# Key pages from GpSimd's DMA queue with the keys dealt eight ways, value pages from the sync engine's

## The chip, the core and the metric

The kernel runs on one core of a Trainium2 chip. A core has a matrix engine (TensorE, PE in the profile, with its weight loads as PEld), a vector engine (VectorE, DVE), an activation engine (ScalarE, ACT), a general engine (GpSimd, POOL), and a sync engine (SP), which here only issues DMAs. DMAs issued from SP, ACT and POOL run on the core's 16 DMA engines and move data between HBM and the on-chip memory of 128 partitions (SBUF). The metric is the device time of one execution in microseconds; lower is better.

## What is computed

One step of a two-layer decoder trunk: layer 0 has stick-breaking attention, layer 1 a diagonal state-space layer; each is followed by a gated MLP with a short convolution. The same weights serve a prompt of 512 tokens and 8 sample sequences of 8 new tokens. The change is in the attention of the samples, whose past of 2048 tokens lies in pages of 128 keys and values:

```python
def stick_breaking_block(q, k, v, bias, q_start):
    z = einsum("bqhd,bkhd->bhqk", q, k) * HEAD_DIM ** -0.5 + bias
    causal = k_pos[None, :] < q_pos[:, None]
    log_keep = where(causal, log_sigmoid(-z), 0.0)
    between = cumsum(log_keep, axis=3, reverse=True) - log_keep
    weights = where(causal, exp(log_sigmoid(z) + between), 0.0)
    return einsum("bhqk,bkhd->bqhd", weights, v)
...
past_kv = [(cache_k[j][page_table].reshape(db, n_pages * PAGE_SIZE, N_HEADS, HEAD_DIM),
            cache_v[j][page_table].reshape(db, n_pages * PAGE_SIZE, N_HEADS, HEAD_DIM))
           for j in range(N_ATTN)]
```

8 sequences, 16 pages each, 128 keys a page, 16 heads of 64: each page is 512 KB of keys and 512 KB of values in fp32, so 67 MB of keys and 67 MB of values are read.

## The kernel before

The sequences are taken in pairs. `sample_cache` (L395) is a generator that walks over 64 steps: 4 pairs, and in each the 16 pages from the last to the first. A step takes one page of both sequences. Its parts are these.

- `load_k` (L406) loads the keys of a step into a tile `kp` of 128 partitions x 4 x 512 floats, two of them (`KBUF`). For each sequence s it reads the page number into a register (`page_id`, L390) and issues two DMAs, one for each half j of the heads, from the sync engine. Each writes 32 partitions, starting at 32 * (2 * j + s): partition kk of the group takes the four keys 4 * kk to 4 * kk + 3. The source's dimensions are 32 x 4 x 512.
- `load_v` (L417) loads the values of a step into a tile `vp` of 128 partitions (one key each) x 2 x 1024 floats, two of them (`VBUF`), with two DMAs from GpSimd. A `vp` buffer comes free when the matmul `po` (L483) of two steps before has read it.
- `turn` (L424) transposes `kp` on VectorE in blocks of 32 x 32 (L427), in two calls a step; after the second, the buffer is free and the keys of two steps on are issued.
- z (L448): 32 matmuls a step with the queries as weights. The output is written so that z's columns are in the order of the keys: out of a column (b, k) to column 4 * k + b.
- ScalarE takes two sigmoids of z, VectorE a reversed running product over the keys and a multiply (`sg`, L464), PE transposes the weights (L473), and `po` (L483) accumulates the weighted values over the 16 pages.

This stream of steps is woven into the prompt's work: `accompany(stream, WEAVE)` lets it take one of its four parts a step after every 2400 columns of the prompt's matmuls. It begins in the first projections (L768), runs beside the prompt's attention (8 pairs of heads, `project_pair`, `norm_pair`, `prompt_pair`) and is finished in the output projection and the first MLP.

The sync engine also issues all weight loads (`load_unit`, L151, its DMA on L168) into three buffers `raw`; ScalarE and VectorE split each into a high and a low part, the first few on GpSimd (`GUNITS`, L140). It issues the prompt's stores as well. An engine issues its DMAs in the order of its program, and one that waits for a buffer holds up those behind it. A scheduler puts each engine's program in order at build time; `tc.issue_after(x)` adds that what is issued in its block on x's engine comes after x. With `raws["last"]` such an order is kept among the weight loads: after the first key loads it is set to the last of their DMAs (L771, `RL` is 2), so that the head pairs' weights come after them on the sync engine.

Of the kernel before, what the change touches and what calls it, by code (L numbers as in the profile page):

```python
# [17 lines left out]
P = 128  # L18
# [35 lines left out]
SB = {"gemm": 3, "tr": 2, "vy": 3}  # L54
SHARE = {"up": "vy"}
EARLY = 2
RL = 2
XA, XB = 0, 2
RAWU = 3, 4
QGROUPS = [[0, 1], [2, 3]]  # L60
# [31 lines left out]
def hybrid_kernel(  # L92
# [9 lines left out]
    V, S, G, T, SP = nc.vector, nc.scalar, nc.gpsimd, nc.tensor, nc.sync  # L102
# [46 lines left out]
    raws = {"pool": glob, "bufs": NRAW, "n": -1, "last": None, "chain": True, "views": {}}  # L149
# [50 lines left out]
    def norm_rows(xs, rows, gain, room=rows_tile, inplace=False):  # L200

        hs = [room()] * len(xs) if inplace else [room() for x in xs]
        ss = const.tile([P, len(xs)], F32, name="ss", tag="ss", bufs=3)
        for i, x in enumerate(xs):
            S.activation(hs[i][:rows], x, AF.Square, accum_out=ss[:rows, i:i + 1])
        r = rsqrt(const, ss, len(xs), rows, 1.0 / D, "nr", 3)
        if inplace:
            hs = xs
        for i, x in enumerate(xs):
            V.scalar_tensor_tensor(hs[i][:rows], x, r[:rows, i:i + 1], gain[:rows], ALU.mult, ALU.mult)  # L210
        return hs
# [86 lines left out]
    def attention_layer(sp, sps):  # L298
# [54 lines left out]
        Qall = sp.tile([P, DB // 2, 16, 32], F32, name="Qall", bufs=1)  # L353
# [34 lines left out]
        last_dma = {}  # L388

        def page_id(eng, idx):  # L390

            with tc.issue_after(last_dma[eng].ins) if eng in last_dma else nullcontext():
                return eng.value_load(idx, min_val=0, max_val=cache_k.shape[1] - 1)

        def sample_cache():  # L395

            steps = [(b, m) for b in range(DB // 2) for m in range(NPG - 1, -1, -1)]
            kps, kts, vps = {}, {}, {}
            prev = po = before = None

            def number(i, s):
                b, m = steps[i]
                n = (2 * b + s) * NPG + m
                return pt[0:1, n:n + 1]

            def load_k(i):  # L406
                if i < len(steps):
                    kps[i] = sp.tile([P, 4, 512], F32, name="kp", tag="kp", bufs=KBUF)
                    for s in range(2):
                        r = page_id(SP, number(i, s))  # L410
                        page = cache_k[0, bass.ds(r, 1)].rearrange("o (kk kb) (j h) d -> j (o kk) kb (h d)", j=2, kb=4)

                        for j in range(2):
                            x = 2 * j + s
                            last_dma[SP] = SP.dma_start(kps[i][32 * x:32 * x + 32], page[j])

            def load_v(i):  # L417
                if i < len(steps):
                    vps[i] = sp.tile([P, 2, D], F32, name="vp", tag="vp", bufs=VBUF)
                    for s in range(2):  # L420
                        r = page_id(G, number(i, s))
                        last_dma[G] = G.dma_start(vps[i][:, s], cache_v[0, bass.ds(r, 1)].rearrange("o k h d -> (o k) (h d)"))  # L422

            def turn(i, a):  # L424
                if i < len(steps):
                    kts[i, a] = sp.tile([P, 4, 8, 32], F32, name="kt", tag="kt")
                    V.transpose(kts[i, a].rearrange("p b c k -> p b (c k)"), kps[i][:, :, a * 256:(a + 1) * 256])  # L427
                    if a:
                        kps.pop(i)
                        load_k(i + KBUF)  # L430

            for i in range(KBUF):
                load_k(i)
            yield
            load_v(0)
            for a in range(2):
                turn(0, a)
            for i in range(len(steps) + 1):
                if i < len(steps):
                    b, m = steps[i]  # L440
                    start = m == NPG - 1

                    z = sps.tile([P, 512], F32, name="z", tag="sz", bufs=2)
                    for a in range(2):
                        kt = kts.pop((i, a))
                        for half in range(2):
                            for h in range(4):
                                T.matmul(z[32 * h:32 * h + 32, a * P:(a + 1) * P].rearrange("p (k b) -> p b k", b=4),  # L448
                                         Qall[:, b, 8 * a + 2 * h + half, :], kt[:, :, 2 * h + half, :], start=half == 0, stop=half == 1)
                        turn(i + 1, a)  # L450
                        if not a:
                            yield
                    sg = sp.tile([P, 2, P], F32, name="sg", tag="sg")

                    left = sp.tile([P, 2, P + 1], F32, name="left", tag="left")
                    for a in range(2):
                        S.activation(left[:, a, :P], z[:, a * P:(a + 1) * P], AF.Sigmoid, bias=nbias_r[:, a:a + 1], scale=-0.125)  # L457
                    for a in range(2):
                        S.activation(sg[:, a], z[:, a * P:(a + 1) * P], AF.Sigmoid, bias=bias_r[:, a:a + 1], scale=0.125)
                    V.memset(left[:, :, P:], 1.0)  # L460
                    for a in range(2):
                        back = left[:, a][:, ::-1]
                        V.tensor_tensor_scan(back, back, back, 1.0 if start else prev[:, a, 0:1], ALU.mult, ALU.min)
                    V.tensor_tensor(sg, sg, left[:, :, 1:], ALU.mult)  # L464
                    prev = left
                    now = i, b, m, z, sg
                    yield
                else:
                    now = None
                if before:  # L470
                    i0, b0, m0, z0, sg0 = before
                    for a in range(2):
                        T.transpose(z0[:, (2 + a) * P:(3 + a) * P], sg0[:, a], ident)  # L473
                    wT = sp.tile([P, 2, P], F32, name="wT", tag="wT", bufs=1)
                    S.copy(wT.rearrange("p e f -> p (e f)"), z0[:, 256:])
                    yield
                    if m0 == NPG - 1:
                        po = sps.tile([P, 2, 256], F32, name="po", tag="so")
                    v = vps.pop(i0).rearrange("p s (j a h d) -> p a h s j d", j=2, a=2, h=4)
                    for a in range(2):  # L480
                        for h in range(4):

                            T.matmul(po[32 * h:32 * h + 32, a].rearrange("p (s j d) -> p s j d", s=2, j=2),  # L483
                                     wT[:, a, 32 * h:32 * h + 32], v[:, a, h],
                                     start=m0 == NPG - 1 and a == 0, stop=m0 == 0 and a == 1)
                    if m0 == 0:
                        for a in range(2):
                            o = sp.tile([P, 256], F32, name="o", tag="wT", bufs=1)
                            S.copy(o, po[:, a])
                            S.dma_start(o_scr[:, b0, a * 256:(a + 1) * 256], o)  # L490
                    yield
                load_v(i + 1)
                before = now

# [216 lines left out]
        with pool_(name="start", bufs=2) as wp, pool_(name="start_ps", bufs=5, space=PSUM) as psp:  # L711
# [9 lines left out]
            with tc.high_priority():  # L721
# [8 lines left out]
                h, = norm_rows([xres[NT][:NS]], NS, gain)  # L730
# [35 lines left out]
            sample_query(1)  # L766
            raws["chain"] = False
            stream = sample_cache()  # L768
            with tc.issue_after(raws["last"].ins) if KAFTER else nullcontext():
                next(stream)  # L770
            raws["last"] = (None, raws["last"], last_dma[SP])[RL]  # L771
            for a in range(2):
                columns("sz", perm, a, lambda x, ps: put_query(x, a, ps))
            for _ in range(HEAD):
# [948 lines left out]
    samp = sctx.enter_context(pool_(name="samp", bufs=2, side="right"))  # L1723
    samp_ps = sctx.enter_context(pool_(name="samp_ps", bufs=1, space=PSUM, side="right"))
    finish_sample, start = attention_layer(samp, samp_ps)

    def between():
# [36 lines left out]
```

## Time and profile before

| | us |
|---|---|
| median of 3 runs | 1864.28 |
| lowest, highest | 1853.79, 1869.25 |
| the profiled execution, its own time | 1861.24 |
| its span | 1859.6 |

The profile is of one execution. Its page gives busy time by engine, the span in 40 slices (each digit is a busy share in tenths; PEclk is the clock granted to TensorE in tenths of full speed; DMA is the mean busy share of the 16 DMA engines), the DMA queues, and the costliest groups of instructions. The trace behind it was asked for stretches of the span, for waits, and for single tiles. q1 is the sync engine's queue, q0 GpSimd's, q10 ScalarE's. A DMA share of a queue is the time that its packets took, as a share of the 16 engines' time in the stretch. A line of "who waited" names the engine and line that sat idle, what it waited for, the total in us, how often, and the longest.

### The profile page before, as it was taken

Reading aid. Unit: us, or ns where it says so; the run is one execution under the profiler, and the core shown is the slowest. Engines: PE = TensorE matmul, PEld = TensorE weight load, DVE = VectorE, ACT = ScalarE, POOL = GpSimd, SP = SyncE. Lnnn points to the kernel's source line nnn. Section 1 sums busy time; section 2 is a strip of 40 time slices with the busy share of each in tenths; the row PEclk is TensorE's granted clock in tenths of the full one; section 3 lists DMA queues with packets and bytes.
Section 4 is the critical chain, followed back from the end, with each engine's and each line's share of the span. In section 5 each row is a group of like instructions: output and inputs, shape, how many; then the busy total and the mean of one; then the engine's idle time right before and its main releaser. Section 6 shows DMA issues by size and latency. Waiting matters only on the chain. (4 is left out here: it accounts for less than half of the span.)

```text
span 1859.6 us, 34131 instructions
## 1 busy us (share of the span) xinstructions
PE 1696.9 (91%) x12765; PEld 1425.3 (77%) x12765; DVE 1157.4 (62%) x2132; ACT 740.9 (40%) x1526; POOL 279.4 (15%) x455
## 2 busy tenths in 40 slices
PE   5979878898788879997999899899999999999999
PEld 4867655566445668796888889789888989989897
DVE  7356755676775567799577887665446544444443
ACT  4324443454453336433244534454433423323231
POOL 3011000111111100066032332011010100000000
PEclk8989988898788989999999999999999999999999
DMA  8399989999999973623375736455322222232221
GB/s 250 97 251 267 252 213 252 257 254 264 275 257 257 255 191 95 181 69 117 113 146 150 199 108 172 120 161 169 118 82 73 91 81 80 81 91 80 82 80 64
DMA packets 278713, 297.30 MB, mean 160 GB/s; under 512 B 54424, under 2 KB 197745, under 8 KB 278548
## 3 DMA queue, kind: packets, MB, share of 16 engines
q1 hardware_dynamic: 258642, 226.66, 45.7%
q0 software_dynamic: 18752, 67.41, 12.9%
q8 instruction: 101, 1.65, 0.4%
q10 hardware_dynamic: 1154, 1.05, 0.2%
q14 instruction: 64, 0.52, 0.1%
HBM read 268.93 MB, written 26.13 MB: 159 GB/s over the span
## 5 line engine op out<-in xcount | busy, mean ns | idle before, releaser
L880 PE MATMUL up<-hT,whi 128*128 128x256 f32 (+2 forms) x1344 | 406.7, 303 | 14.1 <-DVE gf L1000 5.4
L140 DVE TENSOR_TENSOR wlo<-raw,whi 128x1024 fp32r<-128x1024 f32 x203 | 255.2, 1260 | 254.8 <-ACT whi L139 239.4
L881 PE MATMUL up<-hT,whi 128*128 128x256 f32 (+2 forms) x1344 | 402.9, 300 | 0.0
L882 PE MATMUL up<-hT,wlo 128*128 128x256 f32 (+2 forms) x1344 | 402.8, 300 | 0.0
L139 ACT CAST whi<-raw 128x1024 fp32r<-128x1024 f32 x206 | 215.5, 1049 | 335.5 <-PE up L881 152.3
L880 PEld LDWEIGHTS up<-hT,whi 128*128 128x128 f32 x1344 | 256.3, 191 | 22.4 <-DVE gf L1000 7.1
L881 PEld LDWEIGHTS up<-hT,whi 128*128 128x128 f32 x1344 | 256.5, 191 | 3.6 <-issue 0.8
L882 PEld LDWEIGHTS up<-hT,wlo 128*128 128x128 f32 x1344 | 256.2, 191 | 1.6 <-issue 0.2
L427 DVE STREAM_TRANSPOSE kt<-kp 128x1024 f32<-128x1024 f32 x128 | 152.2, 1224 | 156.0 <-DMA kp<-in_cache_k_dram 131.9
L422 POOL DMA_DIRECT2D vp<-in_cache_v_dram x128 | 67.8, 530 | 572.1 <-PE po L483 447.7
L267 PE MATMUL dn<-whi,g 128*128 128x512 f32 x352 | 137.3, 401 | 9.3 <-DVE xres L1077 5.3
L268 PE MATMUL dn<-wlo,g 128*128 128x512 f32 x352 | 140.6, 400 | 0.0
L269 PE MATMUL dn<-whi,g 128*128 128x512 f32 x352 | 139.0, 398 | 0.0
L448 PE MATMUL z<-kt,Qall 128*32 128x128 f32 x2048 | 89.0, 305 | 52.2 <-DVE kt L427 46.6
L448 PEld LDWEIGHTS z<-kt,Qall 128*32 128x32 f32 x2048 | 61.2, 121 | 77.7 <-issue 38.0
L986 POOL COPY cst<-apad 128x2 f32<-128x2 f32 x44 | 39.3, 894 | 510.3 <-ACT apad L974 510.3
L267 PE MATMUL psg<-whi,hT 128*128 128x256 f32 (+1 forms) x320 | 103.2, 325 | 0.0
L268 PE MATMUL psg<-wlo,hT 128*128 128x256 f32 (+1 forms) x320 | 101.9, 319 | 0.0
L269 PE MATMUL psg<-whi,hT 128*128 128x256 f32 (+1 forms) x320 | 100.7, 318 | 0.0
L457 ACT ACTIVATE left<-z,nbias_r 128x128 f32<-128x128 f32 x128 | 40.1, 364 | 146.8 <-PE z L448 128.8
L483 PE MATMUL po<-vp,wT 128*32 128x256 f32 x1024 | 79.8, 432 | 16.5 <-DMA vp<-in_cache_v_dram 11.9
L267 PEld LDWEIGHTS dn<-whi,g 128*128 128x128 f32 x352 | 66.2, 189 | 27.0 <-DVE xres L1077 6.2
(484 smaller groups left out, 3329.9 us busy)
## 6 DMA issues: line engine op xcount, KB each, us to landing
kp<-in_cache_k_dram SPq DMA_DIRECT2D x256, 256.0 KB, 9.1
vp<-in_cache_v_dram POOLq DMA_DIRECT2D x128, 512.0 KB, 9.2
raw<-in_ffn_w_up_dram SPq DMA_DIRECT2D x96, 512.0 KB, 4.4
raw<-in_ffn_w_down_dram SPq DMA_DIRECT2D x48, 512.0 KB, 3.3
raw<-in_attn_w_qkv_dram SPq DMA_DIRECT2D x64, 128.0 KB, 3.6
raw<-in_attn_w_o_dram SPq DMA_DIRECT2D x16, 512.0 KB, 5.4
raw<-in_ssm_w_glu_dram SPq DMA_DIRECT2D x32, 256.0 KB, 3.3
f_scr<-ca SPq DMA_DIRECT2D x8, 512.0 KB
```

Source lines behind the costliest of these rows:

```text
L139: S.copy(hi, src)
L140: eng.tensor_tensor(lo, src, hi.bitcast(F32), ALU.subtract)
L267: T.matmul(ps, x[0], whi, start=st, stop=False)
L268: T.matmul(ps, x[0], wlo, start=False, stop=False)
L269: T.matmul(ps, x[1], whi, start=False, stop=sp_)
L422: last_dma[G] = G.dma_start(vps[i][:, s], cache_v[0, bass.ds(r, 1)].rearrange("o k h d -> (o k) (h d)"))
L427: V.transpose(kts[i, a].rearrange("p b c k -> p b (c k)"), kps[i][:, :, a * 256:(a + 1) * 256])
L448: T.matmul(z[32 * h:32 * h + 32, a * P:(a + 1) * P].rearrange("p (k b) -> p b k", b=4), Qall[:, b, 8 * a + 2 * h + half, :], kt[:, :, 2 * ...
L483: T.matmul(po[32 * h:32 * h + 32, a].rearrange("p (s j d) -> p s j d", s=2, j=2), wT[:, a, 32 * h:32 * h + 32], v[:, a, h], start=m0 == NP ...
L880: T.matmul(ps[:, :t1 - t0], w[0][:, k, :], hi, start=k == 0, stop=False)
L881: T.matmul(ps[:, :t1 - t0], w[0][:, k, :], lo, start=False, stop=False)
L882: last_mm["PE"] = T.matmul(ps[:, :t1 - t0], w[1][:, k, :], hi, start=False, stop=k == KC - 1)
```

## The change

Three things are moved or reshaped. Key DMAs are issued by GpSimd instead of the sync engine. Their source is taken in another order, 8 x 16 x 512: key n * 8 + a of a page goes to place a * 16 + n, so partition p of a group of 32 holds the keys with a = p // 4 and n = 4 * (p % 4) + kb; the outermost dimension is 8. z's output columns are addressed accordingly, so that z itself stays in the order of the keys. Value DMAs are issued by the sync engine. The constant `RL` goes, and `raws["last"]` is the last key DMA, now on GpSimd.

```diff
-RL = 2
@@ load_k
                     for s in range(2):
-                        r = page_id(SP, number(i, s))
-                        page = cache_k[0, bass.ds(r, 1)].rearrange("o (kk kb) (j h) d -> j (o kk) kb (h d)", j=2, kb=4)
-
+                        r = page_id(G, number(i, s))
+                        page = cache_k[0, bass.ds(r, 1)].rearrange("o (n a) (j h) d -> j a (o n) (h d)", j=2, a=8)
                         for j in range(2):
                             x = 2 * j + s
-                            last_dma[SP] = SP.dma_start(kps[i][32 * x:32 * x + 32], page[j])
+                            last_dma[G] = G.dma_start(kps[i][32 * x:32 * x + 32], page[j])
@@ load_v
                     for s in range(2):
-                        r = page_id(G, number(i, s))
-                        last_dma[G] = G.dma_start(vps[i][:, s], cache_v[0, bass.ds(r, 1)].rearrange("o k h d -> (o k) (h d)"))
+                        r = page_id(SP, number(i, s))
+                        last_dma[SP] = SP.dma_start(vps[i][:, s], cache_v[0, bass.ds(r, 1)].rearrange("o k h d -> (o k) (h d)"))
@@ z
-                                T.matmul(z[32 * h:32 * h + 32, a * P:(a + 1) * P].rearrange("p (k b) -> p b k", b=4),
-                                         Qall[:, b, 8 * a + 2 * h + half, :], kt[:, :, 2 * h + half, :], start=half == 0, stop=half == 1)
+                                T.matmul(z[32 * h:32 * h + 32, a * P:(a + 1) * P].rearrange("p (c k a) -> p k a c", c=4, k=4),
+                                         Qall[:, b, 8 * a + 2 * h + half, :], kt[:, :, 2 * h + half, :].rearrange("p k (a c) -> p k a c", c=4), start=half == 0, stop=half == 1)
@@ after the first key loads
-            raws["last"] = (None, raws["last"], last_dma[SP])[RL]
+            raws["last"] = last_dma[G]
```

## Rows read from the trace of the kernel before

**Rows 1.** The page: busy time by engine, and the slices of 46.5 us.
```profile
PE 1696.9 (91%) x12765; PEld 1425.3 (77%) x12765; DVE 1157.4 (62%) x2132; ACT 740.9 (40%) x1526; POOL 279.4 (15%) x455
...
PEclk8989988898788989999999999999999999999999
DMA  8399989999999973623375736455322222232221
```

**Rows 2.** Stretches: length; busy us (count) of PE, PEld, DVE, ACT, POOL; clock, DMA share, GB/s.
```profile
100.00:690.00 590.00, 494.68 (x4961) 346.67 (x4960) 382.72 (x729) 242.41 (x662) 64.63 (x124) 0.87 0.99 251
690.00:1859.00 1169.00, 1120.98 (x7342) 1013.91 (x7341) 717.56 (x1279) 457.21 (x792) 196.90 (x312) 0.99 0.39 112
...
375.00:425.00 50.00, 46.96 (x493) 33.70 (x493) 38.87 (x69) 25.79 (x69) 5.27 (x10) 1.00 1.01 256
```

**Rows 3.** Waits of PE and DVE, 100 to 690 us: total us, times, longest.
```profile
PE z L448 <- DVE kt L427: 46.6, 27, 5.3
PE po L483 <- DMA vp<-in_cache_v_dram: 11.9, 6, 5.3
...
DVE kt L427 <- DMA kp<-in_cache_k_dram: 130.6, 32, 9.4
```

**Rows 4.** Groups of instructions in 100 to 690 us: busy us, mean ns, idle before.
```profile
L448 PE MATMUL z<-kt,Qall 128*32 128x128 f32 x1952 | 85.8, 307 | 52.2 <-DVE kt L427 46.6 <-DVE hn_ss L124 4.5 <-DVE left L460 0.5
...
L464 DVE TENSOR_TENSOR sg<-sg,left 128x256 f32<-128x256 f32 x61 | 25.3, 414 | 1.8
```

**Rows 5.** DMA queues (packets, MB, share): 26-30, 15-22, 500-600, 669-676 us.
```profile
q1 hardware_dynamic: 514, 0.93, 99.0%
...
q1 hardware_dynamic: 1140, 2.00, 83.3%
...
q1 hardware_dynamic: 7237, 13.45, 57.0%
q0 software_dynamic: 3306, 12.06, 42.5%
...
q0 software_dynamic: 288, 1.05, 40.5%
```

**Rows 6.** Tile kp, lines L448 and L691: duration ns min/median/max, first and last start.
```profile
L415 SPq DMA_DIRECT2D kp<-in_cache_k_dram x256: 563/572/5330, 23.2 to 653.9; - x128
L427 DVE STREAM_TRANSPOSE kt<-kp x128: 1199/1233/1247, 31.0 to 666.4; 128x1024 f32<-128x1024 f32 x128
...
L448 PE MATMUL z<-kt,Qall x2048: 269/273/424, 83.5 to 675.6; 128*32 128x128 f32 x187
...
L691 PE MATMUL pz<-ident,psg x160: 270/273/477, 163.0 to 574.8; 128*128 128x128 f32 x160
```

**Rows 7.** Tile vp: its DMAs on POOL, their waits, time to landing.
```profile
L422 POOL DMA_DIRECT2D vp<-in_cache_v_dram x128: 527/527/687, 29.5 to 668.8; - x128
...
DMA to landing us min/median/max: 3.5/9.2/13.4
...
POOL vp L422 <- PE po L483: 447.7, 57, 27.2
```

**Rows 8.** In order of time, POOL and SP: start, us, what, idle before.
```profile
26.36 3.15 POOL L140 TENSOR_TENSOR wlo<-raw,whi 128x1024 fp32r<-128x1024 f32 x1 [1.31 <-ACT whi L139]
...
96.72 0.53 POOL L422 DMA_DIRECT2D vp<-in_cache_v_dram  x1 [0.66 <-issue]
...
23.22 7.91 SPq L415 DMA_DIRECT2D kp<-in_cache_k_dram  x8
31.23 9.09 SPq L168 DMA_DIRECT2D raw<-in_attn_w_qkv_dram  x8
```

**Rows 9.** Waits of the sync engine's queue, 100 to 690 us.
```profile
SPq L415 <- DMA kp<-in_cache_k_dram: 76.3, 43, 4.5
SPq L415 <- DVE left L463: 63.6, 23, 6.7
```

**Rows 10.** Tile raw in 100 to 700 us: who waited for it.
```profile
ACT whi L139: 4.9, 1
```

## The prediction
> **What bounds the kernel now.** I read the page's header and its slices first. TensorE (PE) is busy 91% of the span, but the DMA digit stands at 9, once at 8, from the third slice to the fourteenth and PE's clock has digits 7 to 9 there, against 9 to the end [rows 1]. So the kernel has two regimes, and I cut the span at 100 and 690 us [rows 2]. In the last 1169 us PE is busy 1120.98 at a granted clock of 0.99, with the DMA engines at 0.39: that part is PE's and the change does not touch it. In the 590 us between 100 and 690 the DMA engines are at 0.99 and move 251 GB/s, while PE is busy 494.68 at a mean granted clock of 0.87: the mean lies between the two levels (2.4 and 1.2 GHz), so PE spent parts of the stage at the lower one.
>
> Next, who waits there [rows 3]. PE's largest labelled wait is z (L448) for the transposed keys, 46.6 us, then po (L483) for values, 11.9. The transposes on VectorE (DVE, L427) wait 130.6 us for key pages to land. So the chain is page, transpose, z: data is late, not arithmetic. One `sg` multiply (L464) runs per step, and 61 of them lie in the stage [rows 4]: 590 / 61 = 9.7 us per step.
>
> Then why 251 GB/s is all there is. Three stretches [rows 5]. (a) 26 to 30 us: only the sync queue moves data, the key pages, 0.93 MB at a share of 99.0%: 233 GB/s, or 235 at full share. (b) 15 to 22 us: qkv weights, by the code also in pieces of 2 KB, 2.00 MB at 83.3%: 286 GB/s, or 343 at full share. (c) 500 to 600 us: keys and values together. The software queue (values) takes 42.5% of 16 engines' 100 us for 12.06 MB: 12.06 MB / 680 us = 17.7 GB/s an engine, 284 for 16. The hardware queue, nearly all keys there, takes 57.0% for 13.45 MB: 14.7 GB/s an engine, 236 for 16. (d) When the last values load with weights and no keys (669 to 676 us), values take 40.5% of 7 us for 1.05 MB: 23.1 an engine, 370 for 16. So key pages move at 235 GB/s alone, and values drop from 370 to 284 beside them. What a key DMA has that a weight DMA has not is its target: 32 partitions against 128, all engines writing into the same quarter of the memory.
>
> **The change, part by part.**
>
> *Keys' shape.* The same 256 DMAs of 256 KB in pieces of 2 KB go out; no byte is saved. The outermost dimension becomes 8 runs of 16 keys, each run going into 4 neighbouring partitions, and the two halves of a page (j) go to groups 64 partitions apart. The trace shows no DMA of this form. Bounds: 235 GB/s (nothing changes, [rows 5] a) and 343 (keys move like weights in equal pieces, [rows 5] b). I take 343, with values at 370 (d), since piece size and source are those of fast rows and only the sharing of targets differs. 251 GB/s x 590 us = 148 MB; 61 steps of 1.05 MB are 64 MB of values, 173 us at 370; the other 84 MB at 343 are 245 us. Together 418 us of DMA where 590 were needed. DMA stops being the bound.
>
> The Trainium skill (DMA: Bandwidth & Descriptors, the section on why a DMA increments its semaphore by 16) says that a DMA uses the largest number of engines up to 16 that divides the outermost sizes on both sides, and that GpSimd's DMAs then take consecutive engines from a cursor that goes round, where the hardware queues always start from the first. By it each key half would run on 8 engines and the two halves on different ones, which is the upper bound above; no row here shows which engines a DMA used.
>
> *What becomes the bound.* PE next. The z matmul takes 273 ns at its median and 307 on average in the stage [rows 4, 6]; the difference is the lower clock. 494.68 x 273 / 307 = 440 us of PE work at full clock. PE's idle time is 590 - 494.68 = 95.3 us; less the two waits for pages (58.5) 36.8 remain. How the clock answers: in 375 to 425 us PE was busy 46.96 of 50 and was granted 1.00 [rows 2]; I take 0.95 as a value between 0.87 and that. 440 / 0.95 + 36.8 = 500 us; at 1.00 it would be 477, and with half of the remaining idle time gone too 458. DVE has 382.72 us of work there [rows 2], 77% of 500: below PE. So the stage goes from 590 to 500: 90 us off.
>
> *Keys on GpSimd (POOL).* Four issues a step. From the rows of the value DMAs there [rows 7, 8]: 0.53 us each and 0.66 between two, 4.8 us a step, 290 us in the stage: POOL has the room. It has nothing else in that stage than the value DMAs that leave it [rows 2, 7]. A key buffer comes free when the second transpose ends and is needed two steps on. Round: issue 4.8, landing 3.5 to 9.2 (values from POOL, [rows 7]), two transposes of 1.22 [rows 6]: 10.7 to 16.4 us for two buffers, 5.4 to 8.2 a step, against 500 / 61 = 8.2. It fits, without room to spare at the far end. Cost taken: nothing.
>
> *Values on the sync queue (SP).* Two issues a step of about 0.57 us [rows 6]. POOL waited 447.7 us for po before issuing values, 57 times, the longest 27.2 [rows 7]; that wait moves to SP, and behind it stand the prompt's weight loads and the stores. Until now SP waited there for the key buffers: L415's two largest waits in the stage are 76.3 and 63.6 us [rows 9]. Nothing in the stage waited long for weights: the one wait of ScalarE for a raw weight tile is 4.9 us [rows 10]. Bounds: 0, and a mean value wait (447.7 / 57 = 7.9 us) for each of the 8 head pairs, 63 us. I take 0, nearer to the 4.9.
>
> *Start.* The first 8 key DMAs no longer stand behind SP's weight loads; POOL may put them among its four splits, the last from 26.36 to 29.5 us [rows 8]. 8 x 0.6 us to delay a split is the bound on one side; on the other SP's weight loads of 31 us come 7.91 us earlier [rows 8]. I take +1 us. With `raws["last"]` now on another engine, SP's order after it is free; no price of its own.
>
> *z.* The output is written with runs of 4 at a step of 32 elements instead of 32 at a step of 4; the moving side is read in the same order. L448 with its step of 4 and L691 without a step have the same 273 ns [rows 6]: steps cost nothing visible. Above: doubled, 1.4 us a step (85.8 us busy over 61 steps, [rows 4]). I take 0.
>
> **Sum.** The profiled execution took 1861.24 us for a span of 1859.6; the three runs have a median of 1864.28. 1861.24 - 90 + 1 = 1772; on the scale of the median, 3 higher: 1775.
>
> **Rivals.**
> 1. *The change does not do what it says:* both halves still get in each other's way and keys stay at 235. Then the stage stays at 590 us and the time at 1855 to 1870. For it: no row shows a DMA of this form. The Trainium skill's page SBUF — State Buffer (the section on issuing two DMAs to hit both halves) says that two DMAs at partitions 0 and 64 gained only 6% over one; by it keys would go to 249 GB/s. Against it: (a) and (b) differ in nothing but the targets.
> 2. *The key round on POOL becomes the bound, slower than before.* If each issue is held up by a DVE instruction in progress (a transpose, 1.22 us), a round takes 4.9 us more, 15.6 to 21.3 us, up to 10.6 a step: 61 x 10.6 = 647 us, 57 more than now, 1918. It decides from a round of 19.3 us (9.7 a step). Against it: POOL's value DMAs took 527 ns at least and in the median and 687 at most, amid a DVE busy 65% of the time [rows 2, 7]. The Trainium skill (SBUF — State Buffer, two separate sides) warns that descriptors written by GpSimd starve under some DVE copies; the 687 does not show it for these.
> 3. *Half the gain:* DMA is relieved, but SP behind the values, the DVE queue or the order of PE's program takes part of it back: 1772 + 63 = 1835, between 1800 and 1850.
>
> **How the numbers follow.** Forecast (1724 to 1800) 0.58; rival 3 0.14; rival 1 0.16; rival 2 0.12, of it 0.10 above 1880. A measurement of this kernel can tell about 1% from no change, 1846 to 1883. Faster: 0.58 + 0.13 = 0.71; same: 0.01 + 0.16 + 0.02 = 0.19; slower 0.10. The likeliest one's own range goes down to 1724, halfway between a stage of 458 us (1733 on the median's scale) and one of 440 without any idle time (1715), and up to 1800, where rival 3 begins; the range to hold 8 in 10 reaches into rival 1: 1724 to 1862.
>
> **What would show it.** Right: in the stage the DMA share falls below 0.9 at over 280 GB/s, the software queue moves keys at over 300 GB/s at full share, DVE's wait for kp falls from 130.6 to under 50 us, the clock there rises above 0.93. Rival 1: DMA still at 0.99 and 250 GB/s. Rival 2: POOL issues longer than 0.7 us, or kp waits grow while DMA is not full. Rival 3: SP waits for po with ScalarE waiting for raw tiles. The forecast fails most easily in the step from 590 to 500: that PE alone sets the pace once the pages come in time.

## The result and the profile after

The changed kernel takes 1752.33 us (median of 4 runs, 1750.25 to 1757.19) against 1863.86 (4 runs): a ratio of 0.9411, 95% interval 0.9366 to 0.9456, faster by 5.9%. 1775 was predicted, with a likeliest range of 1724 to 1800. The profiled execution took 1757.19 us for a span of 1755.2.

The medians differ by 111 us, the spans of the two profiled executions by 104. Where these went is read by cutting both spans at the last `po` matmul, which ends the stream of pages: near 684 us before and near 584 us after. Stretches of the kernel before, then of the changed one; the columns are those of [rows 2].

```profile
100.00:685.00 585.00, 492.29 (x4950) 344.28 (x4948) 378.77 (x716) 240.49 (x659) 64.63 (x124) 0.87 0.99 252
685.00:1859.00 1174.00, 1123.38 (x7351) 1016.30 (x7351) 721.51 (x1291) 459.13 (x796) 196.90 (x312) 0.99 0.39 113
```
```profile
0.00:100.00 100.00, 82.07 (x470) 64.19 (x474) 59.82 (x125) 41.07 (x72) 27.16 (x35) 0.95 0.55 180
100.00:585.00 485.00, 453.45 (x4981) 324.98 (x4981) 384.85 (x726) 242.14 (x664) 151.84 (x236) 0.95 0.90 305
585.00:1755.00 1170.00, 1121.99 (x7321) 1016.05 (x7319) 711.78 (x1282) 456.04 (x790) 199.99 (x312) 0.99 0.38 112
```

The stage between holds the same work on PE (4981 matmul instructions against 4950) and is 100 us shorter, 485 instead of 585. The rest is 4 us shorter, which is no more than runs differ. Within the stage the DMA engines now move 305 GB/s instead of 252; PE idles 31.6 us instead of 92.7, and it does the same work in 39 us less busy time, at a granted clock that rose from 0.87 to 0.95: busy time multiplied by the clock is 428 us before (492.29 x 0.87) and 431 after (453.45 x 0.95). So 61 us came from idle time, 50 of them from the two waits for pages, and 39 from the clock.

The waits, PE's and VectorE's, in that stage of the changed kernel, to be held against [rows 3] (engine, line, what it waited for, total us, times, longest):

```profile
PE po L483 <- DMA vp<-in_cache_v_dram: 7.3, 5, 2.4
...
PE z L448 <- DVE kt L427: 1.6, 4, 0.6
...
DVE kt L427 <- DMA kp<-in_cache_k_dram: 20.6, 10, 4.4
```

z's wait for transposed keys went from 46.6 to 1.6 us, and the transposes' wait for key pages from 130.6 to 20.6.

Then the DMA queues, 100 to 580 us: packets, MB, share of 16 engines. First the kernel before, where keys are on q1 (four fifths of its bytes; the rest are weights and stores) and values on q0, then the changed kernel, where keys are on q0 and values on q1, beside weights and stores.

```profile
q1 hardware_dynamic: 50932, 67.08, 58.1%
q0 software_dynamic: 14766, 53.74, 40.3%
```
```profile
q1 hardware_dynamic: 47463, 83.42, 51.8%
q0 software_dynamic: 34136, 62.26, 37.7%
```

Before, q1 needed 58.1% of 16 x 480 us for 67.08 MB: 15.0 GB/s an engine, 241 for 16. After, the keys' queue moves 62.26 MB in 37.7%: 21.5 an engine, 344 for 16. The other queue, values and weights now, rose as well: 21.0 an engine, 335 for 16, where values had 17.4 an engine (278) beside the old key loads.

Last the instructions themselves, as in [rows 6, 7]: duration in ns min/median/max.

```profile
L415 POOL DMA_DIRECT2D kp<-in_cache_k_dram x256: 647/647/845, 21.8 to 559.2; - x128
...
DMA to landing us min/median/max: 3.3/6.5/11.5
...
L448 PE MATMUL z<-kt,Qall x2048: 272/273/423, 83.3 to 573.1; 128*32 128x128 f32 x187
...
L422 SPq DMA_DIRECT2D vp<-in_cache_v_dram x128: 332/333/844, 34.0 to 572.7; - x128
```

A key DMA lands 6.5 us after its issue where it took 9.1. z with its new output order still takes 273 ns.

### The profile page after: what moved, and what is told of

Same layout as the page of the kernel before. It is cut to its first block, busy times and chain, and to the rows that moved or that the text cites. A ratio compares the mean times of both kernels' runs of the same rounds, so it can differ in the third digit from the quotient of the medians.

```text
span 1755.2 us, 34213 instructions
## 1 busy us (share of the span) xinstructions
PE 1657.5 (94%) x12765; PEld 1405.2 (80%) x12765; DVE 1156.4 (66%) x2132; ACT 739.3 (42%) x1526; POOL 379.0 (22%) x583
## 5 line engine op out<-in xcount | busy, mean ns | idle before, releaser
L880 PEld LDWEIGHTS up<-hT,whi 128*128 128x128 f32 x1344 | 257.9, 192 | 21.5 <-DVE gf L1000 8.0
L415 POOL DMA_DIRECT2D kp<-in_cache_k_dram x256 | 166.1, 649 | 360.8 <-DVE kt L427 190.9
L427 DVE STREAM_TRANSPOSE kt<-kp 128x1024 f32<-128x1024 f32 x128 | 152.1, 1222 | 42.2 <-DMA kp<-in_cache_k_dram 20.6
L266 PE MATMUL psg<-whi,hT 128*128 128x256 f32 (+1 forms) x320 | 100.7, 317 | 0.1
L268 PE MATMUL psg<-whi,hT 128*128 128x256 f32 (+1 forms) x320 | 98.0, 309 | 0.0
L266 PEld LDWEIGHTS dn<-whi,g 128*128 128x128 f32 x352 | 66.1, 189 | 24.6 <-DVE xres L1077 5.5
L483 PE MATMUL po<-vp,wT 128*32 128x256 f32 x1024 | 73.4, 404 | 9.5 <-DMA vp<-in_cache_v_dram 7.3
L268 PEld LDWEIGHTS dn<-whi,g 128*128 128x128 f32 x352 | 66.5, 189 | 15.5 <-DVE g L1016 0.3
L267 PEld LDWEIGHTS dn<-wlo,g 128*128 128x128 f32 x352 | 66.6, 189 | 15.3
```

The costliest lines, as they stand in the source:

```text
L266: T.matmul(ps, x[0], whi, start=st, stop=False)
L267: T.matmul(ps, x[0], wlo, start=False, stop=False)
L268: T.matmul(ps, x[1], whi, start=False, stop=sp_)
L415: last_dma[G] = G.dma_start(kps[i][32 * x:32 * x + 32], page[j])
L880: T.matmul(ps[:, :t1 - t0], w[0][:, k, :], hi, start=k == 0, stop=False)
```

## Experiments

Theory A: a key DMA of the old form puts 16 engines on 32 partitions, where they get in each other's way; dealt by 8 and taken in turns, 8 engines go to one group and 8 to another, and nobody shares. Rival B: GpSimd's queue is what is faster. Rival C: the new order of reading the HBM is what is faster. To tell these apart, each half of the change was measured alone, then the same DMAs in another order, and the loads by themselves.

**The swap of queues alone.** The changed kernel with the keys in their old order:

```diff
-  page = cache_k[0, bass.ds(r, 1)].rearrange("o (n a) (j h) d -> j a (o n) (h d)", j=2, a=8)
+  page = cache_k[0, bass.ds(r, 1)].rearrange("o (kk kb) (j h) d -> j (o kk) kb (h d)", j=2, kb=4)
...
-  T.matmul(z[...].rearrange("p (c k a) -> p k a c", c=4, k=4), ..., kt[...].rearrange("p k (a c) -> p k a c", c=4), ...)
+  T.matmul(z[...].rearrange("p (k b) -> p b k", b=4), ..., kt[...], ...)
```

> The two queues are swapped as in the change (keys from GpSimd, values from the sync engine), but the keys keep their old order: outermost dimension 32. Theory A, shared targets (all 16 engines write into one group of 32 partitions and get in each other's way): keys still move at about 235 GB/s at full share, the DMA share stays at 0.99 through the stage, 1840 to 1870 us. Rival B, the queue (GpSimd's queue moves pieces of 2 KB faster, its packets hold 4 KB): the whole gain, about 1752. Rival C, the order of reading (runs of 16 keys 8 apart suit the HBM better): no gain, 1840 to 1870.

Measured: 1858.42 us against 1865.52, ratio 0.9957 (0.9919 to 0.9995). The stage (its last `po` starts at 691.5 us), the two queues in 100 to 580 us, and PE's waits for pages:

```profile
100.00:690.00 590.00, 480.46 (x4981) 341.59 (x4980) 385.81 (x724) 242.66 (x663) 130.55 (x238) 0.88 1.01 251
...
q1 hardware_dynamic: 36128, 66.79, 52.3%
q0 software_dynamic: 16088, 52.74, 46.4%
...
PE po L483 <- DMA vp<-in_cache_v_dram: 78.1, 21, 11.6
...
PE z L448 <- DVE kt L427: 4.7, 9, 1.3
```

The DMA engines are full again at 251 GB/s, and keys from GpSimd move 52.74 MB in 46.4% of 7680 us: 14.8 an engine, 237 for 16, as from the sync engine before. Rival B falls. What the swap does change is who is late: PE now waits 78.1 us for values and 4.7 for keys, where it had been 11.9 and 46.6 [rows 3]. Which of two loads is late is set by the queues; the length of the stage hardly is, 592 us from 100 us to the last `po` against 584.

**The dealing alone.** The kernel before with the keys dealt by 8, still from the sync engine (z's columns addressed accordingly):

```diff
-  page = cache_k[0, bass.ds(r, 1)].rearrange("o (kk kb) (j h) d -> j (o kk) kb (h d)", j=2, kb=4)
+  page = cache_k[0, bass.ds(r, 1)].rearrange("o (n a) (j h) d -> j a (o n) (h d)", j=2, a=8)
```

> The keys are dealt with the outermost dimension 8 as in the change, but still come from the sync engine, and values from GpSimd. Theory A: a DMA takes 8 engines; if the sync queue always takes the same 8, these carry all keys: 61 steps of 512 pieces of about 84 to 95 ns over 8 engines are 330 to 370 us, with half of the values 163 more and weights, some 530 to 580 us in a stage of 585: 1800 to 1865 us, with a DMA share near 0.7. Were the 8 engines taken in turns, about 1752. Rival B: 1864. Rival C: about 1752.

Measured: 1918.54 us against 1865.52, ratio 1.0293 (1.0253 to 1.0334): slower. That is 54 us above the expected range's end. The stage, to its own last `po`, PE's largest wait in it, and the values' queue in 100 to 580 us:

```profile
100.00:742.00 642.00, 495.81 (x4960) 344.14 (x4959) 382.48 (x723) 242.90 (x662) 64.87 (x124) 0.85 0.74 231
...
PE z L448 <- DVE kt L427: 95.6, 34, 9.6
...
q0 software_dynamic: 13798, 50.23, 34.1%
```

The DMA share is 0.74 and yet the stage is longer than before: what is waited for keeps only a part of the engines busy, which the loads by themselves, below, show as a share of a half. Rival C's 1752 us is missed, but a queue that is confined to a part of the engines could hide a faster order of reading; the next experiment, where each DMA reads as in the change, is the one that decides. Theory A is borne out in kind for a queue that does not take engines in turns. My price for it was too low. It had every piece on the 8 engines at its undisturbed time, and values too: these moved 50.23 MB in 34.1% of 7680 us, 307 GB/s for 16 engines, so that the stage's 64 MB take 208 us where 163 were put. Where the rest went was not followed further.

**The same DMAs, half by half.** The changed kernel, with a step's four key DMAs in the order of j, then s, so that DMAs that follow each other go to partitions 0 and 32, then 64 and 96, instead of 0 and 64, then 32 and 96:

```diff
+  pages = []
   for s in range(2):
       r = page_id(G, number(i, s))
-      page = cache_k[0, bass.ds(r, 1)].rearrange("o (n a) (j h) d -> j a (o n) (h d)", j=2, a=8)
-      for j in range(2):
+      pages.append(cache_k[0, bass.ds(r, 1)].rearrange("o (n a) (j h) d -> j a (o n) (h d)", j=2, a=8))
+  for j in range(2):
+      for s in range(2):
           x = 2 * j + s
-          last_dma[G] = G.dma_start(kps[i][32 * x:32 * x + 32], page[j])
+          last_dma[G] = G.dma_start(kps[i][32 * x:32 * x + 32], pages[s][j])
```

> The change with the four key DMAs of a step in another order: both sequences' first half (partitions 0 to 31 and 32 to 63), then both second halves (64 to 95 and 96 to 127); each DMA is the same. Theory A with engines taken in turns by eights: two DMAs that follow each other no longer go to groups 64 apart; if 0 to 31 and 32 to 63 share the same way into the memory, keys fall back to about 235 GB/s and the time to 1830 to 1865. If it is enough that a DMA's 8 engines don't share partitions, about 1752. Rivals B and C: about 1752.

Measured: 1836.05 us, ratio 0.9858 (0.9808 to 0.9909). Three quarters of the gain are gone although each DMA is the same. The two queues in 100 to 580 us:

```profile
q1 hardware_dynamic: 38250, 71.03, 50.1%
q0 software_dynamic: 30748, 56.11, 49.8%
```

Keys: 56.11 MB in 49.8%, 14.7 an engine, 235 for 16. Rival C falls: every DMA still reads in the change's order. So it is not enough that a DMA's own engines keep apart: DMAs that follow each other into groups 32 apart are slow, into groups 64 apart they are not. One rival to the groups is left. In this order neighbours also read two pages instead of the two halves of one. Weights, in pieces of 2 KB as well, moved 343 GB/s [rows 5], which speaks against it, but no run has the one without the other. That the whole is still 22 us faster than the swap alone goes with the values' queue, 295 GB/s at full share here and 266 there; why it suffers less was not tested.

**The loads by themselves.** Nothing of the computation is left: seven stretches, one after the other, of 8 MB of pages each.

> Nothing of the computation is left: seven stretches, one after the other, each loading 8 MB into 8 buffers with no other traffic. Keys in the old order from the sync engine, the same from GpSimd, keys dealt by 8 from the sync engine, the same from GpSimd, the same with both sequences' first half ahead of the second, then values from the sync engine and from GpSimd. Rates over the DMA share. Theory A: 235 GB/s for both stretches in the old order; dealt by 8 from the sync engine under 200 GB/s at a share of at most 0.5; dealt by 8 from GpSimd 340 or more; half by half about 235; values 370 from either. Rival B: the old order from GpSimd 340 or more. Rival C: all three dealt stretches 340 or more at full share.

Measured, from the middle of each stretch (length; busy us of VectorE and GpSimd; clock; DMA share; GB/s):

```profile
15.00:35.00 20.00, 0.00 (x0) 0.00 (x0) 1.00 1.07 224
55.00:75.00 20.00, 0.00 (x0) 9.75 (x18) 1.00 1.04 234
95.00:125.00 30.00, 0.00 (x0) 0.00 (x0) 1.00 0.52 196
140.00:155.00 15.00, 0.00 (x0) 12.03 (x20) 1.00 0.98 319
175.00:200.00 25.00, 0.00 (x0) 12.99 (x21) 1.00 1.06 217
217.00:230.00 13.00, 0.00 (x0) 0.00 (x0) 1.00 1.02 409
242.00:255.00 13.00, 0.00 (x0) 3.97 (x8) 1.00 1.01 404
```

In order: the old form from the sync engine 224 GB/s, from GpSimd 234; dealt by 8 from the sync engine 196 with the DMA engines half busy; dealt by 8 from GpSimd 319; the same half by half 217; values 409 from the sync engine and 404 from GpSimd. Divided by the share, as the expectation has it, they are 209, 225, 377 (of half the engines), 326, 205, 401 and 400. This is theory A's table in its order, not in all sizes: 209, 225 and 205 lie 4 to 13% below its 235, 326 below its 340, and the values above its 370. In the fourth, GpSimd was issuing for 12.03 of the 15 us, so that this stretch is also near the limit of one queue's issues. The half share of the third line shows that on that queue the DMAs with 8 outermost runs keep to half of the engines.

The Trainium skill (SBUF — State Buffer, the section on issuing two DMAs to hit both halves) says that two DMAs at partitions 0 and 64 brought 6% over one. Here both forms send DMAs to partitions 0 and 64 in turns from GpSimd; the old one moves 234 GB/s, the dealt one 319, 36% more: the measurement decides, for DMAs of 8 outermost runs from GpSimd. The rule that these take 8 engines each in turns is the Trainium skill's too (DMA: Bandwidth & Descriptors, why a DMA increments its semaphore by 16); the third, fourth and fifth stretches agree with it, while no row names the engines.

**Together, and other dealings.** Page loads beside each other without the computation, and keys dealt by 16 and by 4:

> Nothing of the computation is left: four stretches of page loads, one after the other. 8 MB of keys dealt by 16 from GpSimd; 8 MB dealt by 4 from GpSimd; then 8 MB of keys in the old order from the sync engine together with 8 MB of values from GpSimd; then 8 MB of keys dealt by 8 from GpSimd together with 8 MB of values from the sync engine. Theory A: by 16 about 235 GB/s; by 4 between 200 and 300 (four ways into the memory an engine pair shares some of the time); together in the old order about 250 GB/s at a full DMA share, as in the kernel's stage; together dealt by 8 at least 330. If page loads beside values were slowed by something that only the whole kernel has, the third stretch would exceed 300.

```profile
15.00:40.00 25.00, 0.00 (x0) 9.86 (x18) 1.00 1.04 231
60.00:85.00 25.00, 0.00 (x0) 14.68 (x19) 1.00 0.86 222
100.00:140.00 40.00, 0.00 (x0) 4.22 (x8) 1.00 1.04 298
165.00:190.00 25.00, 0.00 (x0) 7.32 (x12) 1.00 1.04 389
```

The two queues in the third stretch, 100 to 140 us:

```profile
q0 software_dynamic: 2183, 7.96, 68.4%
q1 hardware_dynamic: 2157, 3.95, 35.4%
```

Keys by 16: 231 GB/s, as in the old form. By 4: 222 at a share of 0.86, so 258 at full share. Keys and values together: 298 GB/s in the old form, 389 dealt by 8. The 298 lies above the expected 250, and just below the 300 that was to show something at work that only the whole kernel has. Two thirds of what moved in that stretch were values (7.96 MB of 11.91), a richer mix than the kernel's. That is not all of the difference: at the kernel's own rates, 241 for keys and 278 for values, this mix would take 45 us and move at 265. What else slows the loads in the kernel stays open.

In the kernel the dealing by 16 and by 4 was made by changing the constants alone (in load_k a=16, in z c=2; by 4, a=4 and c=8):

```diff
-  ..."o (n a) (j h) d -> j a (o n) (h d)", j=2, a=8)
+  ..."o (n a) (j h) d -> j a (o n) (h d)", j=2, a=16)
```

> The change with the keys dealt by 16 instead of 8: from GpSimd, runs of 8 keys, each run into 2 neighbouring partitions. Theory A (what counts is that no two engines write into the same four partitions): 16 engines again write into 32 partitions, two into each four, so keys fall back to about 235 GB/s and the time to 1835 to 1870. Rival C (the order of reading, or any dealing, is what helps): about 1752.

> The change with the keys dealt by 4: runs of 32 keys, each into 8 neighbouring partitions, 4 engines to a DMA if the rule by the outermost dimension holds, the four DMAs of a step on four different sets of engines. Theory A: within a DMA no two engines share four partitions, but the two sequences' DMAs, in flight together, go to groups 32 apart on different engines, which half by half showed to collide: between 1752 and 1836, about 1790. If only a DMA's own engines mattered: about 1752. If few engines to a DMA slow it (a landing of twice the time): above 1800.

Measured: by 16, 1856.24 us, ratio 0.9949 (0.9911 to 0.9987), the swap's time; by 4, 1916.90, ratio 1.0283 (1.0232 to 1.0334). The stretch of 100 to 690 us in each, by 16 first, then by 4. By 16 this is the stage (last `po` at 689.3 us); by 4 the stage goes on to 743.2. Under each stands the keys' queue in 100 to 580 us:

```profile
100.00:690.00 590.00, 483.34 (x4995) 341.88 (x4994) 387.27 (x729) 243.45 (x664) 130.38 (x238) 0.88 1.01 252
...
q0 software_dynamic: 16117, 52.81, 46.4%
```
```profile
100.00:690.00 590.00, 474.36 (x4615) 323.12 (x4613) 355.49 (x654) 226.71 (x622) 180.28 (x225) 0.84 0.99 232
...
PE z L448 <- DVE kt L427: 57.4, 26, 6.3
PE po L483 <- DMA vp<-in_cache_v_dram: 38.9, 15, 8.4
...
q0 software_dynamic: 49979, 48.56, 45.4%
```

By 16 came out as theory A has it. By 4 did not: 1790 was expected. The DMA engines are full at 232 GB/s, and a key DMA lands 11.8 us after its issue instead of 6.5. Alone the form still makes 258 at full share; in 100 to 580 us of the kernel its queue moves 48.56 MB in 45.4%, 223, so part of the loss comes in the company of the values. One difference is on record beside the engines: there the queue moves 49979 packets for 184 key DMAs, some 270 a DMA, against 146 by 8 and 80 by 16. Whether the engines or the packets cost more was not shown, and this stays open.

**What of the change was needed.** Values back on GpSimd, all else as changed; and the change without its last line:

```diff
-  r = page_id(SP, number(i, s))
-  last_dma[SP] = SP.dma_start(vps[i][:, s], ...)
+  r = page_id(G, number(i, s))
+  last_dma[G] = G.dma_start(vps[i][:, s], ...)
```

> The change with the value loads put back on GpSimd, so that GpSimd issues both. Theory 1 (the gain is the key DMAs' targets; values move at 404 to 409 GB/s from either queue): most of the gain stays, 1755 to 1800 us; what is lost is lost by key issues standing behind a value issue that waits for po. Rival (moving the values to the hardware queue brought a good part of the gain): 1800 to 1850.

```diff
-            raws["last"] = last_dma[G]
```

> The change without its last line: the head pairs' weights stay ordered behind the weight load before them on the sync engine instead of being free. Theory: no price, 1745 to 1760 us. Rival (the freed order lets weights come earlier): 1765 or more.

Measured: 1751.88 us, ratio 0.9393 (0.9370 to 0.9416), and 1754.18, ratio 0.9397 (0.9372 to 0.9422). Both are the change's time, the first 3 us below what was expected. The gain is the keys' alone: that values moved to the sync engine, and that the weights' order was freed, has no part in it that these runs can tell.

**Who sets the pace now.** In one run the values of every second step are left out, whose `po` reads the tile of the step before; in another the steps are woven in more densely:

```diff
-                if i < len(steps):
+                if i < len(steps) and i % 2:
+                    vps[i] = vps[i - 1]
+                elif i < len(steps):
```

> The change with the values of every second step left out (that step's po reads the tile of the step before): 32 MB less to move, the same instructions on PE. Theory (after the change PE sets the pace of the stage, DMA has room): 0 to 15 us faster than the change, 1737 to 1752, with the DMA share in the stage falling from 0.90 to about 0.72. Rival (DMA still sets the pace): 32 MB at 343 GB/s are 93 us, the stage falls to about the work of PE, 440 us: 1700 to 1715.

```diff
-WEAVE, NPERIOD, IPERIOD = 2400, 6000, 1200
+WEAVE, NPERIOD, IPERIOD = 2000, 6000, 1200
```

> The change with the steps woven in more densely: one part of a step after every 2000 columns of the prompt's matmuls instead of 2400. If PE sets the pace: within 1%, 1735 to 1770. If page loads still set it, the steps, asked for 17% earlier, wait more and nothing is gained: 1752 to 1790.

Measured: with half of the values 1766.35 us, ratio 0.9459 (0.9432 to 0.9485); with 2000 columns 1752.61, ratio 0.9393 (0.9362 to 0.9424). The stage of the first, and what is behind it:

```profile
100.00:585.00 485.00, 451.88 (x4891) 322.73 (x4890) 383.37 (x731) 240.62 (x664) 151.72 (x235) 0.94 0.75 237
585.00:1766.00 1181.00, 1129.40 (x7413) 1023.42 (x7411) 714.84 (x1277) 454.61 (x788) 197.83 (x313) 0.99 0.39 111
```

32 MB less take the DMA share from 0.90 to 0.75 and give nothing back: PE is as busy as before, and idle for 33.1 us instead of 31.6. DMA has ceased to set the pace. The forecast of 0 to 15 us faster was missed all the same: the kernel became 14 us slower. Its last `po` starts at 577.6 us, 7 us before the change's 584.4, and the loss lies behind that. There PE has 7413 matmul instructions instead of 7321, about as many more as the stage has fewer (4891 instead of 4981), and is busy 7.4 us longer: work has moved to behind the stage. Why it costs more there is open. Weaving more densely changes nothing, as expected where PE sets the pace.

One attempt at something better put values back on GpSimd and wove after every 2200 columns:

> Values back on GpSimd and the steps woven in after every 2200 columns, as an attempt at a version that beats the change: with PE as the pace 1740 to 1755; if page loads still set it, 1755 to 1790.

Measured: 1752.60 us, ratio 0.9396 (0.9348 to 0.9444). No version here beats the change; the one with values back equals it.

## Why the prediction was right, point by point

- *What bounds the stage.* Right. With the keys' loads relieved the stage fell by 100 us, and little else moved: from the last `po` on, 1171 us remain (1755.2 - 584.4) against 1176 before. The same subtraction gives 1171 to 1175 for the swap alone and the dealings by 4 and by 16, and 1180 for the dealing alone and half by half. So the times of these versions differ by the length of this stage, to within 9 us.
- *The keys' rate.* Of the bounds 235 and 343 the upper one was taken; in the kernel it is 344. It was chosen by a likeness to weights, said to differ in nothing but the targets; a weight DMA there is 512 KB and a key DMA 256, which was overlooked. The experiments give the better reason: half by half and the dealing by 16 fall to 235 and 237 with the same bytes, queue and DMA size. That neighbours go to groups 64 apart was no part of the change, as the prediction's wording could suggest; the kernel before had that order, and half by half shows that it is needed. That the rate met the weights' to 1 GB/s is luck: alone the same loads made 326 at full share.
- *DMA time.* 418 us were worked out, 0.90 x 485 = 437 were used. The keys came as priced; values were put at 370 GB/s, and their queue, with the weights, made 335.
- *From 590 to 500.* The stage is 485 us for the 585 between 100 and 685, 100 off where 90 were forecast. PE's busy time was put at 463 (440 at a clock of 0.95) and is 453, its idle time at 36.8 and is 31.6; the forecasts are for a stretch to 690 and hold 5 us more. The clock is 0.95 as taken, but the value was taken between two rows without a rule for it, so that its fit is luck. The sum, 1772 for the profiled execution, was 15 us above its 1757.19: 10 in this stage, 4 behind it, 1 in the start. The forecast was 23 too high, since 3 us were added for the median and the median lies 5 below the profiled execution.
- *POOL's issues.* Sized at 0.53 us each; a key DMA takes 0.65. It did not matter: a round had room, and rival 2 did not come about. GpSimd waited 186.3 us in the stage for key buffers to come free, so it was early, not late.
- *SP behind the values.* The wait that moved was 447.7 us on POOL and is 141.5 on SP. Why it is so much shorter is not shown; that the stage no longer waits for keys is not the reason, since with the swap alone, in a stage as long as before, it is 102.9. ScalarE waited once for a raw weight tile in 100 to 600 us, 1.4 us, where it had been 4.9. The zero was right, and with the values back on GpSimd the time is the same.
- *z's order and the start.* 273 ns as before, and the first 100 us as before (PE busy 82.07 against 81.22, 470 matmul instructions against 466). POOL did put the first key DMAs among its splits, at 21.77 and 25.61 us, without a price.
- *A sign that was off.* The DMA share was to fall below 0.9 and is 0.90: DMA is relieved by less than the rate suggests, because as much is moved in less time (147 MB in 585 us, 148 in 485).

## What to carry to other kernels

Where DMA engines are full below the rate that the same chip reaches elsewhere in the profile, compare the targets before the sources: loads into 32 partitions moved 235 GB/s at full share, loads into 128 moved 343 and more. Loads that must go to groups of 32 partitions can be issued as DMAs with 8 outermost runs, from GpSimd, in an order in which neighbours lie 64 partitions apart (here they were also the two halves of one page); the 8 runs without GpSimd cost 3%, GpSimd without the 8 runs gave 0.4%, and both without the order 1.4% of the 5.9. And relief that big is worth more than the waits it ends: 39 of the 100 us came from the granted clock, which rose from 0.87 to 0.95 when PE's idle share of the stage fell from 16% to 7%.

## What the hardware showed that was not expected

- Loads into a crowded group slow the others too: beside the old key form values fell from 404 GB/s alone to 278, and with the queues swapped to 266 (weights among them), where beside the dealt keys the same queue made 335. With the queues swapped values, not keys, were what PE waited for (78.1 us).
- A key DMA's time on GpSimd follows its outermost dimension: 552 ns at 32 and at 16, 647 at 8, 802 at 4, for the same 256 KB.
- The sync engine issues a value DMA of 512 KB in 333 ns, and a key DMA of 256 KB in the old form in 572 [rows 6], dealt by 8 in 774.
- Fewer outermost runs can be worse than the crowding of the old form: dealt by 4 from GpSimd, and by 8 from the sync engine, the kernel lost 3%.
